# Three PSUM tiles of one bank for the seven-product projections of a hybrid decoder layer

## The chip, the cores and the metric

The kernel runs on one core of a Trainium2 chip. The core has a matrix engine (TensorE, "PE" in the profile, with its weight loads as "PEld"), VectorE ("DVE"), ScalarE ("ACT"), GpSimd ("POOL") and SyncE ("SP"), which here issues every DMA transfer. Each engine works through its own queue of instructions in order; semaphores make one engine wait for another. The metric is the device time of one execution in microseconds, and it is compared by the median of several executions.

## What is computed

One decoder layer on x of 1024 tokens by 1024 features, all in float32, with two token mixers side by side:

```
h      = RMSNorm(x)
q | k | v | z_a | xBC | z_s | dt | gate_logits = h @ w_in
y_a    = differential_attention(q, k, v) * silu(z_a)          # 1024 wide
y_s    = group_norm(state_space(conv(xBC), dt) * silu(z_s))   # 2048 wide
merged = sigmoid(g_a) * (y_a @ w_proj_attn) + sigmoid(g_s) * (y_s @ w_proj_ssd)
out    = x + merged @ w_out
```

The change concerns the line of `merged`: a product with K = 1024 (attention rows) and one with K = 2048 (state-space rows), each gated, then added.

## The kernel before, in words

Every float32 operand of a large product is split into a high and a low part (ScalarE copies the high part, VectorE or GpSimd subtracts it to get the low one), and three matmuls, high by high, high by low and low by high, replace one (`steps3`). Work before the projections is not touched by the change: eight attention heads, four state-space groups, then `gates`, which writes tanh(g/2) of all gate logits to memory (`gt_d`). Since sigmoid(g) is (1 + tanh(g/2)) / 2, gating a block is one VectorE instruction, (gate + 1) * sum.

**The projections** (`products`). The K of 3072 rows is taken in three chunks of 1024, c = 0, 1, 2: attention, then the two halves of the state-space rows. Within a chunk the 1024 output features are taken in four pairs of 128 (ob = 0, 2, 4, 6), and the tokens in two halves. So a pair is a product of a 2x2 block matrix of weights with a 2x2 block matrix of activations. It is computed with seven block products instead of eight, in the order b11, t2, b21, t3, t1, t4, b22 with the numbers 1, 6, 2, 7, 5, 4, 3 (`ORDER`). A block product is 4 blocks of K by 3 matmuls, 12 matmuls of 128 by 128 by 512, and a pair has 84. The products go to three accumulators in PSUM, `into = {1: x, 6: y, 2: x, 7: y, 5: z, 4: y, 3: z}`; a PSUM bank holds 128 x 512 float32, one accumulator. Before, x and y are the two halves of one tile of two banks (`pxy`), and z is a tile of one bank (`pz`). The order of the tile framework's waits goes by tiles: an instruction that writes any part of a tile waits for the earlier readers of that tile.

After each product `pair_step` does its part of the sums: product 1 is copied to SBUF (`pc`, ScalarE); u6 = pc + y, u7 = pc + y (VectorE, L1288); x after product 2 is output block (0,0); u7 + z is block (1,1) (`c22`, L1295); pc + y after product 4 is block (1,0); u6 + z after product 3 is block (0,1). `BEFORE` names which of these must have been planned before a product may be issued: the copy before product 2, u6 before product 7, u7 before product 4, c22 before product 3. `out_block` then gates the block with a gate loaded from `gt_d` (L1319, tile `gl`), adds for c = 1, 2 what the earlier chunks left in memory (`acc_d`, tile `ac`, the add on GpSimd except in the last pair, L1323), and stores it to `acc_d`; in the last pair of c = 2 it splits it for the output product instead. `pair_loads` issues the loads of gates and old sums at 2.0, 7.5, 10.2 and 12.9 us of planned time into a pair.

**Weights** (`pair_splits`). Each pair needs seven weight combinations. GpSimd forms four sums and differences of raw blocks (tiles `s3`, `rawp`), and each of the seven is split: copies on ScalarE, subtractions on VectorE except two on GpSimd (s3 and the last). Tiles `wp`, nine of them, so weights are split more than a pair ahead.

**Activations** (`prepare`, `sums_of`, `fill`). Sums and differences of the y rows are made on GpSimd once per chunk and kept in memory (`t_d`); `fill` loads 28 pieces per chunk and splits each (ScalarE and VectorE) into a "form" (tiles f0b, f1t and so on, or pieces of hH and hL, which held h before). There is room for 31 forms, and a chunk's forms are given free while its last pair (ob = 6) is computed. So 25 of the next chunk's 28 loads and splits fall into the last pair of one chunk and the first of the next.

**What sets the order.** The kernel is written as generators that a planner (`Plan`) runs in the order of a planned time. Each instruction adds an assumed cost to its engine's clock (`mm`, `act`, `tt`, `stt`, `load`), and a task goes on when its inputs are ready by that clock. The result is a fixed order of instructions per engine; the real waits are those of the tiles. `Slots` count buffers: `scs`, `mms` and `trs` are the three PSUM pools of two tiles each (`pxy` came from `scs`, `pz` from `mms`; `trs`, one bank each, were free at this stage).

After the projections `final` multiplies the merged blocks (`mg`, split by `split_mg`) with w_out into tiles `po` and adds x.

## Time and profile before

| | |
|---|---|
| median of three executions | 1723.9 us (1723.13 to 1725.33) |
| profiled execution | 1722.27 us |
| its span, first to last instruction | 1720.5 us |
| TensorE busy | 1649.6 us, 96% |
| VectorE, ScalarE, GpSimd busy | 1095.6, 814.6, 595.4 us |
| gates end, projections begin | 1338.7 us |
| projections c = 0, 1, 2 | 90.6, 98.8, 99.1 us |
| last matmul of the projections, end of span | 1627.2, 1720.5 us |

The profile gives each engine's busy time, and with every wait what ended it. In a timeline row stand the start and length in microseconds, the engine, the line, the operation with its output and inputs, the number of instructions merged into the row, and in brackets the idle time before it with its releaser. A matmul takes 0.39 us from start to end, but one starts about every 0.23 us, so TensorE's busy share hides short stops; the start times do not.

### The profile page before, as it was taken

To read this page: it belongs to the slowest core of one execution; us is meant where nothing else is said; L and a number is where in the kernel's file an instruction comes from. 1 tells how busy PE (TensorE), PEld (TensorE's weight loads), DVE (VectorE), ACT (ScalarE), POOL (GpSimd) and SP (SyncE) were. 2 spreads that over 40 slices of the span, in tenths; PEclk is the share of its full clock that TensorE was granted. 3 is DMA by queue.
4 is the path that set the end of the run, shared out by engine and by line. 5 is a ranking of instruction groups with operands and counts; after the bars stand their busy time and mean duration, and the time that the engine had idled before them with its cause. 6 is when DMAs were issued, how large, how long until landed. Compare 5 with 4: busy or idle time off the path is not lost. (4 is left out here: it accounts for less than half of the span.)

```text
span 1720.5 us, 23583 instructions
## 1 busy us (share of the span) xinstructions
PE 1649.6 (96%) x8226; PEld 1364.5 (79%) x8226; DVE 1095.6 (64%) x1878; ACT 814.6 (47%) x1967; POOL 595.4 (35%) x656
## 2 busy tenths in 40 slices
PE   7999999999999999999999999999999888877899
PEld 5788888888888888888888888888788666665787
DVE  6676676677676635788588489466641658586621
ACT  5646556556565533564565365255442424142310
POOL 4323233233232210233333233167645344656200
PEclk9999999999999999999999999999999999999999
DMA  6202022021120121321422233077695657586732
GB/s 186 62 10 62 7 56 62 7 56 32 31 62 7 56 68 49 98 80 44 122 80 62 91 100 80 19 227 262 222 339 187 222 192 264 189 281 202 243 130 68
DMA packets 171044, 198.66 MB, mean 115 GB/s; under 512 B 11813, under 2 KB 114990, under 8 KB 170926
## 3 DMA queue, kind: packets, MB, share of 16 engines
q1 hardware_dynamic: 170926, 197.16, 36.0%
q8 instruction: 65, 1.06, 0.3%
q14 instruction: 53, 0.43, 0.1%
HBM read 147.71 MB, written 49.41 MB: 115 GB/s over the span
## 5 line engine op out<-in xcount | busy, mean ns | idle before, releaser
L165 PE MATMUL pma<-w,hH 128*128 128x512 f32 x1024 | 343.4, 405 | 0.2 <-ACT hH L189 0.2
L165 PE MATMUL pc<-hH,w 128*128 128x512 f32 x768 | 243.7, 394 | 0.0
L165 PEld LDWEIGHTS pma<-w,hH 128*128 128x128 f32 x1024 | 189.6, 190 | 34.6 <-ACT hH L189 0.6
L165 PE MATMUL pma<-w,hL 128*128 128x512 f32 x512 | 206.6, 404 | 0.0
L189 ACT ACTIVATE w<-raw 128x512 fp32r<-128x512 f32 (+1 forms) x194 | 120.5, 625 | 125.5 <-PE pc L165 46.3
L194 POOL TENSOR_TENSOR w<-raw,w 128x512 fp32r<-128x512 f32 (+1 forms) x62 | 83.8, 1352 | 260.9 <-ACT w L189 255.6
L165 PE MATMUL pmz<-w,hH 128*128 128x512 f32 x512 | 165.4, 397 | 0.0
L165 PEld LDWEIGHTS pc<-hH,w 128*128 128x128 f32 x768 | 142.9, 188 | 28.2
L165 PE MATMUL pg<-hH,w 128*128 128x512 f32 x512 | 161.9, 393 | 0.0
L194 DVE TENSOR_TENSOR w<-raw,w 128x512 fp32r<-128x512 f32 x132 | 111.1, 848 | 69.6 <-ACT w L189 66.4
L165 PE MATMUL pc<-hL,w 128*128 128x512 f32 x384 | 151.7, 395 | 0.0
L189 ACT ACTIVATE p<-p,nm 128x256 f32<-128x256 f32 (+7 forms) x128 | 98.2, 769 | 46.2 <-DVE nm L645 46.2
L189 ACT ACTIVATE wp<-rawp 128x512 fp32r<-128x512 f32 x72 | 45.1, 631 | 156.4 <-PE pxy L165 82.9
L165 PEld LDWEIGHTS pg<-hH,w 128*128 128x128 f32 x512 | 95.8, 188 | 19.2
L165 PEld LDWEIGHTS pma<-w,hL 128*128 128x128 f32 x512 | 97.2, 190 | 16.9 <-DVE hL L194 0.3
L165 PEld LDWEIGHTS pmz<-w,hH 128*128 128x128 f32 x512 | 94.8, 188 | 18.2
L165 PE MATMUL pmz<-w,hL 128*128 128x512 f32 x256 | 101.0, 395 | 0.0
L165 PE MATMUL pg<-hL,w 128*128 128x512 f32 x256 | 100.9, 394 | 0.0
L199 DVE SCALAR_TENSOR_TENSOR cv<-pc,cols,cv 128x1023 f32<-128x1023 f32 (+2 forms) x72 | 91.8, 1275 | 12.2 <-ACT cv L189 11.5
L645 DVE CUSTOM_DVE_ANT_0 p<-sc,maskb 128x256 f32<-128x256 f32 (+7 forms) x128 | 91.5, 752 | 12.2 <-PE sc L165 11.6
L221 POOL TENSOR_TENSOR f<-ssv,e 128x1 f32<-128x1 f32 x64 | 13.7, 214 | 245.0 <-ACT av L189 245.0
L189 ACT ACTIVATE ab<-ab,nac 128x128 f32<-128x128 f32 x256 | 77.9, 390 | 28.1 <-POOL ab L934 28.1
(252 smaller groups left out, 3628.3 us busy)
## 6 DMA issues: line engine op xcount, KB each, us to landing
raw<-in_w_in_dram SPq DMA_DIRECT2D x176, 256.0 KB, 3.1
ab<-act_d SPq DMA_DIRECT2D x32, 512.0 KB, 5.4
t_d<-ts SPq DMA_DIRECT2D x24, 512.0 KB, 3.4
gl<-gt_d SPq DMA_DIRECT2D x48, 256.0 KB, 4.4
acc_d<-gl SPq DMA_DIRECT2D x44, 256.0 KB, 2.2
ys_d<-xdt SPq DMA_DIRECT2D x32, 256.0 KB, 2.5
gt_d<-gt SPq DMA_DIRECT2D x32, 256.0 KB, 5.4
ts<-ys_d SPq DMA_DIRECT2D x16, 512.0 KB, 5.9
```

The costliest lines, as they stand in the source:

```text
L165: nc.tensor.matmul(o, lhsT=lhsT, rhs=rhs, start=start, stop=stop, **kw)
L189: nc.scalar.activation(o, i, f, **kw)
L194: (nc.vector if eng == "V" else nc.gpsimd).tensor_tensor(out=o, in0=a, in1=b, op=op)
L199: nc.vector.scalar_tensor_tensor(out=o, in0=a, scalar=s, in1=b, op0=op0, op1=op1)
L221: nc.gpsimd.tensor_tensor(out=dst, in0=src, in1=add, op=ALU.add)
L645: nc.vector.tensor_tensor_reduce(out=p[:, 0:n], in0=sc[:, 0:n], in1=maskb[:, S - n:S], scale=-1.0, scalar=3e38, op0=ALU.add, op1=ALU.min, ...
```

## The change

The accumulators x, y and z become three tiles of one bank each: X from `trs`, Y from `mms`, Z from one half of a tile of `scs`. The sums that complete a block are written back to the accumulator in PSUM instead of to SBUF for c = 1, 2: c22 goes to X (after block (0,0) has been gated), block (1,0) to Y, (0,1) to Z; each accumulator is given free after its last gating.

The order of the chunks changes: the two halves of the state-space rows are c = 0 and 1, the attention rows c = 2. For c = 0 nothing is gated and no gate is loaded: the four raw sums are stored to `acc_d` (block (0,0) through a ScalarE copy). For c = 1 the old sum is added and the result gated, once for both halves. For c = 2 the block is gated and the old sum added. The add of the old sum is on VectorE always. The subtraction for the weight s3 moves from GpSimd to VectorE.

The planner's assumed costs change from the projections on: 0.0135 us instead of 0.003 beside a matmul's columns, and 2.5 us instead of 0.8 from a transfer's end to its use. `prepare` no longer waits for the attention rows (they are done long before) but for the first state-space groups.

```diff
+    lag = [0.003, 0.8]
...
-            c = max(n / 2400 + 0.003, 0.057 if m <= 64 else 0.107)
+            c = max(n / 2400 + lag[0], 0.057 if m <= 64 else 0.107)
...
-        return pl.op("D", n, q + 0.6) + 0.8
+        return pl.op("D", n, q + 0.6) + lag[1]
...
-    for src, r0 in ((w_pa, 0), (w_ps, 0), (w_ps, 1024)):
+    for src, r0 in ((w_ps, 0), (w_ps, 1024), (w_pa, 0)):
...
-        t = yield from split(s3, t3, "G")
+        t = yield from split(s3, t3, "V")
...
     def products(c):
         for ob in range(0, 8, 2):
             ids = w_next(7)
-            ks = yield from pl.get(scs)
-            kz = yield from pl.get(mms)
-            sc, z = sct(f"pxy{c}{ob}"), mmt(f"pz{c}{ob}")
-            x, y = sc[:, 0:512], sc[:, 512:1024]
+            ks = []
+            for q in (trs, mms, scs):
+                ks.append((yield from pl.get(q)))
+            x, y, z = trt(f"pX{c}{ob}"), mmt(f"pY{c}{ob}"), sct(f"pZ{c}{ob}")[:, 0:512]
             into = {1: x, 6: y, 2: x, 7: y, 5: z, 4: y, 3: z}
-            cell = {"kc": (yield from pl.get(mids))}
-            pl.spawn(pair_loads(c, ob, cell))
+            cell = {"kc": (yield from pl.get(mids)), "x": x, "ks": ks}
+            if c:
+                pl.spawn(pair_loads(c, ob, cell))
...
         elif p == 2:
-            yield from out_block(c, ob, 0, 0, ps, cell, at)
+            if c:
+                yield from out_block(c, ob, 0, 0, ps, cell, at)
+            else:
+                k = yield from pl.get(mids)
+                o = midt(name=f"o{c}{ob}")
+                at = act(o, ps, AF.Copy, at)
...
         elif p == 5:
...
-            cell["c22"] = at = tt(u, u, ps, ALU.add, max(at, t))
-            yield from out_block(c, ob, 1, 1, u, cell, at)
-            mids.give(k, cell["done", 1, 1])
+            if c == 0:
+                cell["c22"] = at = tt(u, u, ps, ALU.add, max(at, t))
+                yield at
+                at = load(acc_row(ob + 1, 1), u, at)
+                mids.give(k, at)
+                return
             while ("done", 0, 0) not in cell:
                 yield pl.t + 0.1
+            cell["c22"] = at = tt(cell["x"], u, ps, ALU.add, max(at, t, cell["done", 0, 0]))
+            mids.give(k, at)
+            yield from out_block(c, ob, 1, 1, cell["x"], cell, at, (trs, kx))
         else:
...
+            k0, r, h, q, kq = (None, 1, 0, mms, ky) if p == 4 else ("u", 0, 1, scs, kz)
+            u, k, t = (cell["c"], cell["kc"], cell["ct"]) if p == 4 else cell["u", 6]
+            o = ps if c else u
+            at = tt(o, u, ps, ALU.add, max(at, t))
...
-        at = stt(gt, gt, 1.0, src, ALU.add, ALU.mult, at)
+        if c == 1:
+            at = tt(ps, ps, ac, ALU.add, at)
+            at = stt(gt, gt, 1.0, ps, ALU.add, ALU.mult, at - HOP)
+        else:
+            at = stt(ps, gt, 1.0, ps, ALU.add, ALU.mult, at)
+            at = tt(gt, ps, ac, ALU.add, at - HOP)
         cell["done", r, h] = at
-        if c:
-            yield at
-            at = tt(gt, gt, ac, ALU.add, at, "V" if c == 2 and ob == 6 else "G")
...
         yield from gates()
+        lag[:] = [0.0135, 2.5]
         for c in range(3):
             yield from products(c)
```

Three places show how the change moves instructions. Names are tiles with a number; wp is a split weight, f1b, f1t, hH and hL are forms, and what stands in brackets is what the instruction waits for.

TensorE, a quiet pair of c = 1 (ob = 2), the end of product 1, products 6 and 2, and the start of product 7, before:

```order
L165 MATMUL pxy_14069<-f1b_13668,wp_13853 128x512 x3
L165 MATMUL pxy_14069<-f1t_13676,wp_13884 128x512
L165 MATMUL pxy_14069<-f1t_13676,wp_13884 128x512 [waits Activation_49]
L165 MATMUL pxy_14069<-f1t_13676,wp_13884 128x512
L165 MATMUL pxy_14069<-f1t_13682,wp_13884 128x512 x3
L165 MATMUL pxy_14069<-f1t_13693,wp_13884 128x512 x3
L165 MATMUL pxy_14069<-f1t_13703,wp_13884 128x512 x3
L165 MATMUL pxy_14069<-f1b_13709,wp_13919 128x512 x2
L165 MATMUL pxy_14069<-f1b_13709,wp_13919 128x512 [waits DVE_49]
L165 MATMUL pxy_14069<-f1b_13716,wp_13919 128x512 x3
```

The same pair now:

```order
L167 MATMUL pX_14043<-f1b_13643,wp_13828 128x512 x3
L167 MATMUL pY_14044<-f1t_13651,wp_13862 128x512 x3
L167 MATMUL pY_14044<-f1t_13657,wp_13862 128x512 x3
L167 MATMUL pY_14044<-f1t_13665,wp_13862 128x512 x3
L167 MATMUL pY_14044<-f1t_13675,wp_13862 128x512 x3
L167 MATMUL pX_14043<-f1b_13681,wp_13894 128x512 [waits Activation_49]
L167 MATMUL pX_14043<-f1b_13681,wp_13894 128x512 x2
L167 MATMUL pX_14043<-f1b_13687,wp_13894 128x512 x3
L167 MATMUL pX_14043<-f1b_13695,wp_13894 128x512 x3
L167 MATMUL pX_14043<-f1b_13705,wp_13894 128x512 x3
L167 MATMUL pY_14044<-f1t_13711,wp_13919 128x512 [waits DVE_49]
```

The wait for ScalarE's copy of product 1 moved from product 6 to the start of product 2, and the wait for VectorE's u6 from product 2 to the start of product 7: each now has a whole product in front of it. The order of the products is the same.

GpSimd, about the same pair, before:

```order
L194 TENSOR_TENSOR rawp_14041<-rawp_14041,rawp_14042 128x4x128 [waits DMAHW3_49,Pool_49]
L194 TENSOR_TENSOR gl_14141<-gl_14141,ac_14143 128x512 [waits DMAHW3_49,DVE_49]
L194 TENSOR_TENSOR rawp_14041<-rawp_14041 128x4x128 [waits DVE_49,Pool_49]
L194 TENSOR_TENSOR gl_14165<-gl_14165,ac_14167 128x512 [waits DMAHW6_49,DVE_49]
L194 TENSOR_TENSOR gl_14188<-gl_14188,ac_14190 128x512 [waits DMAHW1_49,DVE_49]
L194 TENSOR_TENSOR rawp_14042<-rawp_14042,rawp_14041 128x4x128 [waits DVE_49,Pool_49]
L194 TENSOR_TENSOR wp_14276<-s_14194,wp_14276 128x512 [waits Activation_49]
L194 TENSOR_TENSOR gl_14249<-gl_14249,ac_14251 128x512 [waits DMAHW6_49,DVE_49]
L194 TENSOR_TENSOR wp_14336<-rawp_14042,wp_14336 128x512 [waits Activation_49]
```

Now, from one weight s3 to the pair's last split:

```order
L196 TENSOR_TENSOR s_14160<-rawp_14018 128x512 [waits DMAHW4_49,DVE_49]
L196 TENSOR_TENSOR rawp_14018<-rawp_14018,rawp_14019 128x4x128 [waits DMAHW5_49,Pool_49]
L196 TENSOR_TENSOR rawp_14018<-rawp_14018 128x4x128 [waits DVE_49,Pool_49]
L196 TENSOR_TENSOR rawp_14019<-rawp_14019,rawp_14018 128x4x128 [waits DVE_49,Pool_49]
L196 TENSOR_TENSOR wp_14307<-rawp_14019,wp_14307 128x512 [waits Activation_49]
```

The four adds of old sums and the split of s3 left GpSimd, which has five instructions per pair in place of ten.

VectorE, the pair ob = 4 of c = 1 from u6 on, before:

```order
L194 TENSOR_TENSOR u_14278<-pc_14258,pxy_14230 128x512
L199 SCALAR_TENSOR_TENSOR gl_14249<-gl_14249,pxy_14230 128x512
L194 TENSOR_TENSOR wp_14293<-rawp_14041,wp_14293 128x512
L194 TENSOR_TENSOR u_14317<-pc_14258,pxy_14230 128x512
L194 TENSOR_TENSOR wp_14314<-rawp_14042,wp_14314 128x512
L194 TENSOR_TENSOR u_14317<-u_14317,pz_14231 128x512
L199 SCALAR_TENSOR_TENSOR gl_14295<-gl_14295,u_14317 128x512
L194 TENSOR_TENSOR pc_14258<-pc_14258,pxy_14230 128x512
```

Now:

```order
L196 TENSOR_TENSOR u_14245<-pc_14226,pY_14198 128x512
L196 TENSOR_TENSOR wp_14243<-s_14160,wp_14243 128x512
L196 TENSOR_TENSOR pX_14197<-pX_14197,ac_14218 128x512
L201 SCALAR_TENSOR_TENSOR gl_14217<-gl_14217,pX_14197 128x512
L196 TENSOR_TENSOR wp_14264<-rawp_14018,wp_14264 128x512
L196 TENSOR_TENSOR u_14288<-pc_14226,pY_14198 128x512
L196 TENSOR_TENSOR wp_14286<-rawp_14019,wp_14286 128x512
L196 TENSOR_TENSOR pX_14197<-u_14288,pZ_14199 128x512
L196 TENSOR_TENSOR pX_14197<-pX_14197,ac_14259 128x512
L201 SCALAR_TENSOR_TENSOR gl_14258<-gl_14258,pX_14197 128x512
L196 TENSOR_TENSOR pY_14198<-pc_14226,pY_14198 128x512
```

The adds of the old sums (ac) and the split of s3 came in; a gating now has a PSUM operand where it had an SBUF copy, and the sum c22 (pX from u and pZ) stands behind the gating of block (0,0), whose two inputs gl and ac are loads.

More of the change, by code (lines that the diff above doesn't have):

```diff
@@ L1143, in y_rows @@
     def y_rows(c, kb):
-        return ya_d[kb * P:(kb + 1) * P] if c == 0 else ys_d[(c * 8 - 8 + kb) * P:(c * 8 - 7 + kb) * P]
+        return ya_d[kb * P:(kb + 1) * P] if c == 2 else ys_d[(c * 8 + kb) * P:(c * 8 + kb + 1) * P]
     def prepare():
-        while ready.get("ya", 0) < 2 * HEADS or ready["ya_at"] > pl.t:
+        while ready.get("ssd", {}).get(1, INF) > pl.t:
             yield pl.t + 0.5
         yield from sums_of(0)
-        while ("ssd", 1) not in ready:
-            yield pl.t + 0.5
-        yield from sums_of(1)
-        while ("ssd", GROUPS - 1) not in ready or ready["ssd", GROUPS - 1] > pl.t:
+        yield from sums_of(2)
+        while ready["ssd"].get(GROUPS - 1, INF) > pl.t:
             yield pl.t + 0.5
         pl.spawn(fill())
-        yield from sums_of(2)
+        yield from sums_of(1)
     def sums_of(c):
@@ L1261, in products @@
                 w_done(ids[n])
-                pl.spawn(pair_step(c, ob, p, into[p], cell, ks, kz), pe_done())
+                pl.spawn(pair_step(c, ob, p, into[p], cell), pe_done())
     def pair_loads(c, ob, cell):
@@ L1266, in pair_loads, with acc_row, pair_step @@
             yield pl.t + d
-            grow = ob + r + (8 if c else 0)
-            km = yield from pl.get(mids, 2 if c else 1)
-            km = km if c else [km]
-            gt = midt(name=f"gl{c}{ob}{r}{h}")
+            grow = ob + r + (8 if c == 1 else 0)
+            km = yield from pl.get(mids, 2)
+            gt, ac = midt(name=f"gl{c}{ob}{r}{h}"), midt(name=f"ac{c}{ob}{r}{h}")
             t = load(gt, gt_d[grow * P:(grow + 1) * P, h * 512:h * 512 + 512])
-            ac = None
-            if c:
-                ac = midt(name=f"ac{c}{ob}{r}{h}")
-                t = load(ac, acc_d[(ob + r) * 256 + h * P:(ob + r) * 256 + h * P + P])
+            t = max(t, load(ac, acc_row(ob + r, h)))
             cell["g", r, h] = (gt, ac, km, t)
-    def pair_step(c, ob, p, ps, cell, ks, kz):
+    def acc_row(ob, h):
+        return acc_d[ob * 256 + h * P:ob * 256 + h * P + P]
+    def pair_step(c, ob, p, ps, cell):
         at = pe_done()
+        kx, ky, kz = cell["ks"]
         if p == 1:
@@ L1289, in pair_step @@
         elif p == 2:
-            yield from out_block(c, ob, 0, 0, ps, cell, at)
+            if c:
[4 more added lines that the diff above has]
+                at = act(o, ps, AF.Copy, at)
+                cell["done", 0, 0] = at
+                trs.give(kx, at)
+                yield at
+                at = load(acc_row(ob, 0), o, at)
+                mids.give(k, at)
         elif p == 5:
@@ L1327, in out_block @@
         else:
-            at = load(acc_d[(ob + r) * 256 + h * P:(ob + r) * 256 + h * P + P], gt, at)
+            at = load(acc_row(ob + r, h), gt, at)
             if c == 2:
```

32 lines of the change are left out of this document (15 added, 17 removed).

## The prediction

> **What bounds the kernel now.** First the page's busy shares, then the busy times by stage and by pair of output blocks, then the timeline of one quiet pair, last the waits. In a window row stand length, busy time (and instructions) of PE, PEld, DVE, ACT and POOL, granted clock, DMA share, GB/s. The first three rows are the chunks c=0, 1, 2 of the seven-product projections; the others are pairs, from the first of c=0 to the last of c=2.
>
> ```profile
> PE 1649.6 (96%) x8226; PEld 1364.5 (79%) x8226; DVE 1095.6 (64%) x1878; ACT 814.6 (47%) x1967; POOL 595.4 (35%) x656
> ...
> 1338.70:1429.30 90.60, 79.94 (x339) 62.39 (x338) 62.61 (x78) 36.46 (x65) 34.84 (x24) 1.00 0.64 215
> 1429.30:1528.10 98.80, 82.54 (x342) 64.15 (x341) 70.32 (x85) 31.56 (x56) 55.73 (x39) 0.98 0.70 230
> 1528.10:1627.20 99.10, 82.50 (x331) 62.95 (x330) 67.69 (x82) 32.84 (x57) 49.56 (x33) 0.97 0.66 225
> ...
> 1338.70:1361.30 22.60, 19.97 (x86) 15.60 (x85) 20.81 (x27) 12.82 (x24) 8.10 (x6) 1.00 0.76 256
> 1361.30:1383.90 22.60, 19.90 (x86) 15.52 (x85) 11.03 (x15) 4.91 (x8) 8.79 (x7) 1.00 0.38 126
> 1429.30:1455.00 25.70, 21.74 (x87) 16.84 (x86) 21.14 (x29) 10.18 (x19) 10.19 (x8) 0.93 0.83 281
> 1455.00:1479.00 24.00, 19.65 (x84) 15.22 (x83) 15.70 (x20) 5.43 (x9) 14.75 (x10) 1.00 0.57 175
> 1503.00:1528.10 25.10, 21.13 (x90) 16.48 (x90) 20.99 (x24) 11.15 (x20) 15.51 (x12) 1.00 0.85 280
> 1528.10:1557.00 28.90, 20.85 (x78) 14.86 (x76) 26.11 (x29) 11.61 (x21) 16.33 (x11) 0.94 0.78 269
> 1557.00:1582.00 25.00, 22.25 (x94) 17.30 (x94) 16.00 (x19) 4.91 (x8) 15.76 (x11) 1.00 0.55 181
> 1605.00:1627.20 22.20, 20.37 (x88) 16.13 (x87) 15.57 (x25) 11.53 (x20) 5.14 (x4) 1.00 0.89 308
> ```
>
> TensorE sets the pace, and this stage, 288.5 us from 1338.7 to 1627.2, is where it has holes. What it needs at least comes from a product without a wait, in the chain that ended last; a pair in a timeline shows where a hole is.
>
> ```profile
> 1600.64 2.72 PE pxy L165 x12
> ```
> ```profile
> 1364.15 0.39 PE L165 MATMUL pxy<-f0t,wp 128*128 128x512 f32 x1
> 1364.88 0.58 ACT L189 ACTIVATE pc<-pxy 128x512 f32<-128x512 f32 x1
> 1365.52 2.79 PE L165 MATMUL pxy<-f0t,wp 128*128 128x512 f32 x11 [0.98 <-ACT pc L189]
> 1368.14 0.61 PE L165 MATMUL pxy<-f0b,wp 128*128 128x512 f32 x2
> 1368.87 0.69 DVE L194 TENSOR_TENSOR u<-pc,pxy 128x512 f32<-128x512 f32 x1 [3.16 <-PE pxy L165]
> 1369.61 2.57 PE L165 MATMUL pxy<-f0b,wp 128*128 128x512 f32 x10 [0.85 <-DVE u L194]
> 1372.01 0.61 PE L165 MATMUL pxy<-f0t,wp 128*128 128x512 f32 x2
> 1372.66 0.69 DVE L199 SCALAR_TENSOR_TENSOR gl<-gl,pxy 128x512 f32<-128x512 f32 x1 [3.11 <-PE pxy L165]
> 1373.50 1.86 PE L165 MATMUL pxy<-f0t,wp 128*128 128x512 f32 x7 [0.87 <-DVE gl L199]
> ```
>
> Twelve matmuls start in 2.72 us, 0.2267 each; a pair has 84, so 19.04 us, and the twelve pairs 1008, so 228.5. The stage **loses 60.0 us**. The timeline shows three stops per pair, none wanted by the algorithm: product 6, which goes to y, waits for ScalarE's copy of x; product 2, into x, waits for the DVE sum that reads y; product 7, into y, for the gating that reads x. Both accumulators are one tile pxy, and the dependency is held by the tile. The stops are 1365.52 - 1364.15 - 0.23 = 1.14, 1369.61 - 1368.37 - 0.23 = 1.01 and 1373.50 - 1372.24 - 0.23 = 1.03 us, 3.2 together; the matmuls behind a stop start 0.24 apart ((2.79 - 0.39) / 10), which is the other 0.4 of the pair's 22.6 - 19.04 = **3.56 us**. Twelve pairs: 42.7 of the 60.0. The other 17.3 are the rows longer than 22.6: 3.1 and 2.5 + 6.3 where one chunk's operands replace the other's, 1.4 in the quiet pair of c=1 shown (its neighbour is alike), 2.4 in one of c=2 and 0.4 in the next. In these quiet pairs the copy itself is late:
>
> ```profile
> 1584.18 1.15 ACT L189 ACTIVATE wp<-rawp 128x512 fp32r<-128x512 f32 x2 [5.58 <-POOL rawp L194]
> 1585.24 0.58 ACT L189 ACTIVATE pc<-pxy 128x512 f32<-128x512 f32 x1
> 1585.87 1.22 PE L165 MATMUL pxy<-hH,wp 128*128 128x512 f32 x2 [2.27 <-ACT pc L189]
> ```
>
> The copy is queued on ScalarE behind weight conversions, and these wait for POOL, where four adds of the old sums stand per pair in c=1 and 2.
>
> **Part 1, three tiles of one bank: -42.7.** In the new order every matmul that waits for ScalarE or VectorE has a whole other product (2.72 us) between it and the work that it waits for: the copy has product 6, the sums u6 and u7 have products 2 and 5, the sum that frees z has product 4. In the rows above the reader is done 0.9 to 1.3 us behind the last matmul (1364.54 to 1365.46 for the copy), so it is hidden with over 1 us to spare; without that cover the 1 us stops return. The bounds are 0 and 42.7; I take all of it.
>
> **Part 2, POOL's adds to VectorE, split of s3 too.**
>
> ```profile
> L194 POOL TENSOR_TENSOR gl<-gl,ac 128x512 f32<-128x512 f32 x14 | 21.3, 1530 | 14.8 <-DVE gl L199 14.8
> ...
> L199 DVE SCALAR_TENSOR_TENSOR gl<-gl,pc 128x512 f32<-128x512 f32 x4 | 5.8, 1462 | 0.0
> L194 DVE TENSOR_TENSOR u<-pc,pxy 128x512 f32<-128x512 f32 x8 | 5.5, 686 | 10.2 <-issue 5.3 <-PE pxy L165 4.8
> L194 DVE TENSOR_TENSOR hH<-ry1t,hH 128x512 fp32r<-128x512 f32 x4 | 2.7, 680 | 0.0
> ...
> L194 DVE TENSOR_TENSOR pS<-pS,pre x24: 681/691/700, 728.5 to 1225.7; 128x512 f32<-128x512 f32 x24
> ...
> 1530.87 0.60 DVE u L194
> ```
>
> POOL falls from ten operations per pair to five, so ScalarE's weight conversions there no longer wait behind adds, and the quiet pairs of c=1 and 2 should run like those of c=0: -1.4 x 2 - 2.4 - 0.4 = -5.6. A sum with a PSUM operand costs VectorE 0.69 (writing PSUM too, as pS does), 0.60 where one follows another; an operation with both inputs in SBUF costs the same alone but 1.46 on average beside POOL. c=0: 62.6 us for 78 operations, 12.7 over 0.64 each, by 24 on POOL: half a microsecond each. A quiet pair of c=1 or 2 now has 19 DVE operations, 19 x 0.60 + 5 x 0.5 = 14 of its 19 us: hidden.
>
> The rule against this is in the Trainium skill, "VectorE: DVE Perf Modes", Rules for kernel authors: copy a matmul's output to SBUF first if many operations follow. By it sums left in PSUM are the dear form, and the total could only be above mine. The trace disagrees: by the rows above the PSUM form is 0.69 always and the SBUF form 0.68 to 1.46, and the total keeps 0.60 in a queue.
>
> **Part 3, where the chunks change.** Here 25 forms (operands split in two) pass VectorE while gating runs. By the new order VectorE issues 58 operations over the two pairs at c=0/1 (53 before) and 63 at c=1/2 (51 before). With ten POOL operations at 0.5: 58 x 0.60 + 5 = 39.8 and 63 x 0.60 + 5 = 42.8, against 38.1 us of matmuls: late by 1.7 and 4.7. The transfers press too: the two rows about 1528.1 moved 280 x 25.1 + 269 x 28.9 = 14.8 MB; in 38.1 us that is 388 GB/s, where the highest 20 us row of the trace has 369.
>
> ```profile
> 1260.00:1280.00 20.00, 20.00 (x90) 16.57 (x89) 10.84 (x12) 10.79 (x18) 9.65 (x7) 1.00 1.03 369
> ```
>
> At 369 they need 40.1, late by 2.0 beside the 4.7. The bounds: 0, if weights (split a pair ahead) give way in the queue; and today's 11.9 with 17 more operations at 0.69, 24. I take 2.5 and 5, near the worked rows, and 0.25 for each of the other eight pairs: **9.5 us stay lost of 60.0**. Nothing else on the path is added: c=0 loses its gate loads and gating, and its one extra ScalarE copy takes 0.58 in a queue that is under a third busy there; order of the chunks and later landing times (2.5 for 0.8) only move queue entries.
>
> The clock: after the longest waits it is lower, for some 3 us.
>
> ```profile
> 1534.00:1538.00 4.00, 0.27 (x2) 1.00 0.54 198
> 1538.00:1542.00 4.00, 4.00 (x11) 0.57 0.90 308
> ```
>
> In the pairs at 0.93 and 0.94 above that is 1.8 + 1.7 us, already among the 11.9; I expect one such drop at c=1/2, within the 5. The Trainium skill ("TensorE: Matmul & The Clock Gate", Part 1) gives an idle window of about 3.4 us for it: by that rule waits of 1 to 2 us leave the clock alone, and the term would be 1.7 less.
>
> **Part 4, the tail.** From the stage's end to the span's end it is 93.3 us now.
>
> ```profile
> 1634.15 1.92 PE L165 MATMUL po<-w,hL 128*128 128x512 f32 x6 [1.79 <-ACT hL L189]
> ...
> 1634.15 83.17 PE po L165 x387
> ```
>
> The last pair's VectorE work (15.6 of 22.2 us above) must now end in 19: I add 1.0, between -1.8 (this wait gone) and +3 (the 3.2 us that the pair gets shorter).
>
> **Sum.** 1338.7 + 228.5 + 9.5 + 94.3 = 1671.0 span. The profiled execution is 1.8 above its span (1722.3 to 1720.5), the median 1.6 above that: **1674.4 us**, 49.5 less than 1723.9 (2.9%).
>
> **Rivals.**
> *All covered* (0.18): the chunk changes cost nothing and the po wait goes: 1338.7 + 228.5 + 91.5 + 3.4 = 1662. For it: c=0's first pair took 22.6 with 27 operations on VectorE. Against: 42.8 us of work in 38.1.
> *Queues bound at the chunk changes* (0.20): transfers and VectorE together, the 24 us of part 3, tail +2: 1338.7 + 228.5 + 24 + 95.3 + 3.4 = 1690. For it: DMA share 0.83 to 0.85 already there. Against: POOL's stretching halves.
> *The true waits take over* (0.08): the copy and sums late by over the 2.7 us of cover, as the 2.27 wait shows that ScalarE can be; if half of part 1 returns, 1674.4 + 21 = 1695. The change then does half of what it says. Against: c=0 never had it (0.98).
> *Slower* (0.04): a new chain. The sum that frees z for product 3 now stands behind the gating of block (0,0), and in c=1 and 2 that needs its two loads.
>
> ```profile
> gl<-gt_d SPq DMA_DIRECT2D x47, 256.0 KB, 4.4
> ...
> ac<-acc_d SPq DMA_DIRECT2D x31, 256.0 KB, 5.2
> ```
>
> Product 3 starts 6 x 2.72 = 16.3 us into a pair; three operations (2.1) before it leave 14.2, and the loads are issued at 2: it decides from a landing of 12 us, and a landing of 19 would cost 7 us in each of 8 pairs, 1674.4 + 56 = 1730. Against: the medians are less than half of 12.
>
> **How the numbers follow.** The forecast has 0.50. The range 1662 to 1695 reaches over the rivals but the last. A median here can tell 0.2% from no change; only the last rival can come out there or above: faster 0.95, same 0.01, slower 0.04.
>
> **What would show it.** Part 1: quiet pairs of 19.0 to 19.4 us in all chunks, with the 0.98, 0.85 and 0.87 us of idle time gone. Part 2: POOL under 30 us in each chunk (20 operations, today 24 take 34.8 in c=0), DVE's PSUM sums at 0.69. Part 3: the pairs at c=0/1 and 1/2 over 38.1 by 2.5 and 5. Part 4: po no earlier than 94 us before the end. Wrong if quiet pairs stay above 20, or if the chunk changes lose over 20.

## The result, and the profile after

The changed kernel takes **1678.97 us** (median of four runs, 1677.29 to 1681.57) against 1723.69 for the kernel before (four runs beside it, 1723.13 to 1725.33): a ratio of **0.974 [0.9723, 0.9757]**, 44.7 us less. The forecast was 1674.4, with a range of 1662 to 1695. The profiled execution, the fastest of the four, took 1677.29 us with a span of 1675.5 us (before 1722.27 and 1720.5).

First the busy shares on the page of the changed kernel.

```profile
PE 1638.2 (98%) x8226; PEld 1364.6 (81%) x8226; DVE 1084.8 (65%) x1902; ACT 815.9 (49%) x1971; POOL 530.5 (32%) x616
```

TensorE does the same 8226 matmuls in a span that is 45.0 us shorter. GpSimd lost 40 operations and 65 us. VectorE got 24 operations more and is busy 11 us less.

The busy times by stretch, columns as in the prediction: the chunks c = 0, 1, 2; two quiet pairs (the second of c=0, the third of c=1); the last pair of c=0 and the first of c=1; the last of c=1 and the first of c=2; the last pair of c=2; the tail.

```profile
1338.55:1414.70 76.15, 76.15 (x337) 63.08 (x336) 48.18 (x69) 37.73 (x68) 27.50 (x20) 1.00 0.60 202
1414.70:1504.96 90.26, 80.35 (x337) 64.62 (x336) 74.63 (x104) 33.24 (x58) 30.58 (x22) 0.96 0.81 275
1504.96:1583.77 78.81, 77.29 (x338) 62.76 (x336) 65.73 (x97) 31.57 (x54) 19.58 (x15) 1.00 0.75 252
1357.60:1376.60 19.00, 19.00 (x85) 15.76 (x84) 8.11 (x12) 5.41 (x9) 7.16 (x6) 1.00 0.34 113
1457.90:1476.90 19.00, 19.00 (x85) 15.76 (x84) 12.72 (x19) 4.92 (x8) 6.42 (x5) 1.00 0.68 225
1395.70:1414.70 19.00, 19.00 (x85) 15.74 (x84) 14.96 (x22) 13.77 (x26) 6.77 (x5) 1.00 1.00 342
1414.70:1438.85 24.15, 20.25 (x86) 15.46 (x84) 24.08 (x32) 10.92 (x20) 8.45 (x6) 1.00 0.89 298
1476.90:1504.96 28.06, 22.05 (x85) 17.64 (x84) 22.18 (x34) 12.60 (x22) 8.74 (x6) 0.88 0.93 328
1504.96:1526.64 21.68, 20.16 (x86) 15.46 (x85) 21.51 (x32) 10.76 (x19) 6.68 (x5) 1.00 0.88 291
1564.73:1583.77 19.04, 19.04 (x86) 15.77 (x84) 16.73 (x27) 10.98 (x19) 2.60 (x2) 1.00 0.97 340
1583.77:1675.50 91.73, 88.06 (x409) 73.14 (x407) 23.25 (x35) 8.01 (x13) 3.90 (x3) 1.00 0.35 119
```

A quiet pair now takes 19.0 us where it took 22.6 to 25.0: TensorE is busy in all of it. c=0 has no hole (76.15 for four pairs of 19.04). The stage from 1338.55 to 1583.77 lasts 245.2 us, 43.3 less than before, and loses 16.7 over the 228.5 that its matmuls need. All of that lies in three pairs: 5.1 in the first pair of c=1, 9.0 in the last of c=1, 2.6 in the first of c=2. The tail lasts 91.7 us, 1.6 less than before.

What TensorE waits for from the projections on, in the changed kernel (microseconds in total, times, longest; the largest three):

```profile
PE pY L167 <- DVE u L196: 8.2, 4, 6.0
PE pZ L167 <- DVE pX L196: 1.4, 2, 0.8
PE pX L167 <- ACT pc L191: 1.1, 1, 1.1
...
```

Before, there was a stop in every pair for the copy, for u6 and for a gating. What is left is mostly the wait for u6 or u7 at the two chunk changes, with one long instance.

At the change from c=0 to c=1 the waits in TensorE's timeline of the changed kernel are:

```profile
1421.42 3.01 PE L167 MATMUL pX<-f1b,wp 128*128 128x512 f32 x12 [1.11 <-ACT pc L191]
1425.20 3.01 PE L167 MATMUL pY<-f1t,wp 128*128 128x512 f32 x12 [0.76 <-DVE u L196]
...
1432.12 0.98 PE L167 MATMUL pY<-hL,wp 128*128 128x512 f32 x3 [1.19 <-DVE u L196]
...
1436.01 0.93 PE L167 MATMUL pZ<-hL,wp 128*128 128x512 f32 x3 [0.83 <-DVE pX L196]
```

These are the waits that the algorithm wants (copy before product 2, u6 before 7, u7 before 4, c22 before 3), each with a whole product as cover and still too late. VectorE is busy 24.08 of this pair's 24.15 us: it is the bound here. The first wait, for ScalarE's copy, leads back to it as well: the copy stood behind a weight conversion that waited 3.21 us for GpSimd, and GpSimd had waited 1.89 us for a weight subtraction on VectorE. In the pair ahead of this one VectorE was busy 14.96 of 19.00.

At the change from c=1 to c=2 the long wait is seen with VectorE's and ScalarE's rows:

```profile
1489.85 0.84 PE L167 MATMUL pZ<-hH,wp 128*128 128x512 f32 x3
1490.12 2.49 DVE L196 TENSOR_TENSOR f2b<-ry2b,f2b 128x512 fp32r<-128x512 f32 x4
...
1493.03 1.25 ACT L191 ACTIVATE f2t<-ry2t 128x512 fp32r<-128x512 f32 x2 [0.98 <-DMA ry2t<-t_d]
...
1493.69 2.36 DVE L196 TENSOR_TENSOR f2t<-ry2t,f2t 128x512 fp32r<-128x512 f32 x2 [1.08 <-ACT f2t L191]
...
1495.97 0.67 DVE L196 TENSOR_TENSOR u<-pc,pY 128x512 f32<-128x512 f32 x1
...
1496.70 1.65 PE L167 MATMUL pY<-hL,wp 128*128 128x512 f32 x3 [6.01 <-DVE u L196]
```

Product 5 ends at 1490.7, and product 4 waits 6.01 us for u7 (tile u). u7 is one VectorE instruction of 0.67 us whose inputs were there at 1488.0, when product 7 ended. In the 8.0 us from there to its start VectorE worked through nine instructions ahead of it in its queue, eight of them subtractions for the next chunk's forms. It was idle for only 1.08 us of this, where a form (f2t) waited for ScalarE, which waited for a transfer. So u7's place in the queue makes it late, more than a late operand does. Behind the wait the clock is lower, in the same kernel:

```profile
1496.70:1502.00 5.30, 5.30 (x13) 4.14 (x14) 2.68 (x4) 0.26 (x1) 0.48 (x1) 0.50 1.07 371
```

That is 5.3 us at 0.50, some 2.6 us of the 9.0 that this pair loses.

### The profile page after: what moved, and what is told of

Same layout as the page of the kernel before. It is cut to its first block, busy times and chain, and to the rows that moved or that the text cites. A ratio compares the mean times of both kernels' runs of the same rounds, so it can differ in the third digit from the quotient of the medians.

```text
span 1675.5 us, 23517 instructions
## 1 busy us (share of the span) xinstructions
PE 1638.2 (98%) x8226; PEld 1364.6 (81%) x8226; DVE 1084.8 (65%) x1902; ACT 815.9 (49%) x1971; POOL 530.5 (32%) x616
## 4 chain that ended last, share of the span: by engine, by line
PE 82%; DVE 5%; POOL 4%; issue 4%; ACT 3%; DMA 2%; SPq 0%; POOLq 0%; DVEq 0%; ACTq 0%
PE pma L167 17%; PE pc L167 15%; PE pmz L167 9%; PE pg L167 7%; PE po L167 5%; PE pY L167 4%; PE sc L167 4%; PE av L167 4%; PE pX L167 3%; PE pD L167 3%; PE pZ L167 2%; PE pa L176 2%; POOL ts L196 1%; ACT qh L191 1%; PE pS L167 1%
## 5 line engine op out<-in xcount | busy, mean ns | idle before, releaser
L167 PEld LDWEIGHTS pmz<-w,hH 128*128 128x128 f32 x512 | 94.8, 188 | 18.3
L647 DVE CUSTOM_DVE_ANT_0 p<-sc,maskb 128x256 f32<-128x256 f32 (+7 forms) x128 | 91.5, 752 | 12.2 <-PE sc L167 11.6
```

What stands on the lines that cost most here:

```text
L167: nc.tensor.matmul(o, lhsT=lhsT, rhs=rhs, start=start, stop=stop, **kw)
L647: nc.vector.tensor_tensor_reduce(out=p[:, 0:n], in0=sc[:, 0:n], in1=maskb[:, S - n:S], scale=-1.0, scalar=3e38, op0=ALU.add, op1=ALU.min, ...
```

## The experiments

Each is the changed kernel with one edit, except the first. Beside the median stands the length of the stage, from the first matmul into the first x to the first into `po`, read from the timeline of the kernel's profile: the stage begins at another time in each run, 1337.6 to 1341.0 us, and the stage is free of that. A ratio is to runs of the kernel before that were made beside the experiment (medians 1723.35 to 1725.89), so where kernels of different rows are close, the intervals of their ratios decide.

| kernel | median us (lowest to highest) | ratio to before | stage us |
|---|---|---|---|
| before | 1723.69 (1723.13 to 1725.33) | | 288.5 |
| after | 1678.97 (1677.29 to 1681.57) | 0.974 [0.9723, 0.9757] | 245.2 |
| 1 tiles only | 1683.43 (1682.82 to 1685.31) | 0.976 [0.9746, 0.9775] | 249.3 |
| 2 shared tile | 1744.37 (1743.37 to 1746.31) | 1.0113 [1.0098, 1.0128] | 310.4 |
| 3 old landing time | 1683.25 (1682.31 to 1684.26) | 0.9757 [0.9743, 0.9772] | 249.5 |
| 4 s3 on GpSimd | 1678.0 (1676.2 to 1678.48) | 0.9728 [0.9712, 0.9744] | 244.3 |
| 5 no low halves on VectorE | 1673.23 (1671.77 to 1673.77) | 0.9705 [0.969, 0.9719] | 237.7 |
| 6a landing 4.0 | 1683.33 (1682.31 to 1684.79) | 0.9765 [0.9751, 0.978] | 250.1 |
| 6b landing 5.5 | 1697.22 (1694.4 to 1699.98) | 0.9845 [0.9828, 0.9862] | 267.1 |
| 7 dearer VectorE | 1682.66 (1681.63 to 1683.88) | 0.9759 [0.9742, 0.9775] | 250.2 |
| 8 narrow gates | 1678.11 (1676.83 to 1679.25) | 0.9737 [0.972, 0.9753] | 244.1 |
| 9 last pair kept | 1677.12 (1675.81 to 1678.54) | 0.9731 [0.9717, 0.9746] | 244.6 |
| 10 kept, s3 on GpSimd | 1678.3 (1677.81 to 1680.18) | 0.974 [0.9725, 0.9755] | 246.7 |
| 11 eight adds fewer | 1673.8 (1672.82 to 1676.18) | 0.9716 [0.9703, 0.9729] | 241.6 |

A stage is that of one profile, and the low clock moves it by a microsecond and more: behind the long wait of c=1 it covers 5.8 us of matmuls in the changed kernel, but 2.9 in experiment 4, 3.5 in 8 and 3.7 in 11. Stages that differ by less than that are not told apart.

### 1 and 2: what is the tile split worth, alone and taken back?

Experiment 1 is the kernel before with the three accumulators in three tiles, each given free by itself, and nothing else:

```diff
-            sc, z = sct(f"pxy{c}{ob}"), mmt(f"pz{c}{ob}")
-            x, y = sc[:, 0:512], sc[:, 512:1024]
+            x, y, z = trt(f"pX{c}{ob}"), mmt(f"pY{c}{ob}"), sct(f"pZ{c}{ob}")[:, 0:512]
```

> The kernel before with one edit: the accumulators x, y, z are three tiles of one bank (chunk order, gating on every chunk, the adds on GpSimd and the planner's costs stay). Theory: the shared tile cost 3.56 us per pair, 42.7 in all, and the late copies of c=1, 2 (5.6) are covered too, since a whole product stands before each wait; the chunk changes get tighter by about 5. So 1723.7 - 43 to 1723.7 - 34: 1681 to 1690. Rival A (the gain is in the order of the queues, set by the planner's costs and the chunk order): above 1705. Rival B (the gain is in GpSimd's relief): above 1705, with the copy of product 1 late by 2.3 us in c=1, 2 as before.

Experiment 2 is the changed kernel with x and y back in the halves of one tile (z in `mms`), everything else as changed:

```diff
-            x, y, z = trt(f"pX{c}{ob}"), mmt(f"pY{c}{ob}"), sct(f"pZ{c}{ob}")[:, 0:512]
+            sc, z = sct(f"pxy{c}{ob}"), mmt(f"pz{c}{ob}")
+            x, y = sc[:, 0:512], sc[:, 512:1024]
```

> The changed kernel with X and Y as halves of one tile of two banks again and Z a tile of one bank, all else as changed. Theory: three stops of about 1 us come back in each of twelve pairs, +42.7 at most; the 16.7 us that the changed kernel's projections still lose at the chunk changes get smaller because VectorE has 22.6 instead of 19.0 us per pair: 1705 to 1722. Rival A and B: within 10 us of the changed kernel's 1679.

The split alone came out as expected: 1683.4, stage 249.3, so 39.2 of the stage's 43.3 us. All the rest of the change is worth the other 4.1; the intervals of the two ratios overlap. Its waits of TensorE, from the projections on (the two largest and the one for the copy):

```profile
PE pY L165 <- DVE u L194: 5.2, 5, 2.8
PE pZ L165 <- DVE u L194: 3.4, 2, 2.3
...
PE pX L165 <- ACT pc L189: 0.6, 1, 0.6
```

In the kernel before, the wait for the copy was the largest of its list:

```profile
PE pxy L165 <- ACT pc L189: 18.2, 12, 2.4
```

The wait for the copy, which came twelve times with up to 2.4 us each, is there once, with 0.6, although GpSimd still has its adds. All waits of the stage over 0.2 us lie between 1421 and 1437 and between 1494 and 1529, about the chunk changes, so the quiet pairs are free of them.

Experiment 2 missed. I had expected that the shared tile takes the split's gain back at most; it came out 18.5 us slower than the kernel before that ran beside it (1725.89). The rest of the change is good only with the split. A quiet pair of c=1 in experiment 2:

```profile
1463.60 2.79 PE L178 MATMUL pxy<-f1t,wp 128*128 128x512 f32 x11 [0.98 <-ACT pc L202]
...
1467.69 2.58 PE L178 MATMUL pxy<-f1b,wp 128*128 128x512 f32 x10 [0.85 <-DVE u L207]
...
1472.24 2.56 PE L178 MATMUL pxy<-f1t,wp 128*128 128x512 f32 x10 [1.52 <-DVE gl L212]
...
1478.54 0.73 PE L178 MATMUL pxy<-hL,wp 128*128 128x512 f32 x2 [0.79 <-DVE pxy L207]
...
1481.48 0.96 PE L178 MATMUL pxy<-hL,wp 128*128 128x512 f32 x3 [1.51 <-DVE gl L212]
...
1489.78 1.43 PE L178 MATMUL pxy<-f1t,wp 128*128 128x512 f32 x5 [0.98 <-ACT pc L202]
```

The first three stops are those of before. Two are new: a matmul into y waits for a sum that is now written into x, and for the gating that now reads x. The stop at 1472.24 is longer too (1.52 for 0.87 us), since the add of the old sum now comes ahead of the gating. The pair takes 1489.78 - 1463.60 = 26.2 us, where it took 22.6 to 25.0 before and 19.0 now. Keeping the sums in PSUM makes more readers and writers of each accumulator, and with a shared tile each of them stops its neighbour.

### 3 and 4: the new landing time and s3

```diff
-        lag[:] = [0.0135, 2.5]
```

> The changed kernel with the planner's old costs (0.003 us beside a matmul, 0.8 us after a transfer). Theory: only the order in the queues moves, and a quiet pair has over 5 us of idle VectorE, so quiet pairs stay at 19.0 to 19.5; the chunk changes, where VectorE and the transfers are full, can lose up to 10 more because loads count as landed too early: 1676 to 1692. Rival A (the planner's costs carry the gain): above 1700.

```diff
-        t = yield from split(s3, t3, "V")
+        t = yield from split(s3, t3, "G")
```

> The changed kernel with the split of the weight s3 on GpSimd again (0.60 us per pair less on VectorE, about 1.3 more on GpSimd, which stretches VectorE's SBUF operations by about 0.5). Theory: nothing of this is on the path in a quiet pair and the two effects cancel at the chunk changes: 1676 to 1682. Rival B: more than 1684, with ScalarE's weight conversions waiting for GpSimd again.

Both came within what was expected. The place of s3 makes no difference that can be measured. With the planner's old costs the kernel is 4.3 us slower by the medians and by the stage, though the intervals of the two ratios overlap, and the largest wait is another:

```profile
PE pZ L167 <- DVE pX L196: 7.7, 3, 5.0
...
```

This is product 3 waiting for c22 behind the gating of block (0,0): the mechanism of the prediction's slower rival, with 5.0 us in the first pair of c=2. The planned time of 2.5 us from landing to use keeps it at 1.4 in the changed kernel. It gains nothing at c=1/2, where the last pair of c=1 and the first of c=2 lose 9.5 us together with the old costs and 11.6 now. It gains in the last pair of c=2, which takes 23.6 us with the old costs and 19.0 now, and 1.2 us in the first pair of c=1.

### 5: is it VectorE at the chunk changes?

For c=1 and 2 ScalarE writes both halves of a form in one activation, and VectorE's subtraction for the low half is left out. The low half is then a second copy of the high one: this kernel leaves that part of the computation out.

```diff
-        t = act(form[0][:, 0], raw, AF.Copy, t)
-        yield t
-        t = tt(form[0][:, 1], raw, form[0][:, 0], ALU.subtract, t)
+        if c:
+            t = act(form[0], raw.unsqueeze(1).to_broadcast([P, 2, 512]), AF.Copy, t)
+        else:
+            ...
```

> The changed kernel, but for the chunks c=1, 2 the low part of the activation forms is written by ScalarE's one instruction together with the high part (both halves get the same copy), so that 56 VectorE subtractions are left out: the low part is not computed there. Transfers are the same. Theory: at c=0/1 VectorE is full (24.1 of 24.2 us in the first pair of c=1), at c=1/2 its queue holds sum u7 behind nine form subtractions that wait for late loads. Without them both losses (5.1 and 9.0 us) fall to 3 together: 1666 to 1671. Rival (the transfers themselves are too late, at 0.93 of their time): product 1 of the next chunk waits for its forms instead, 1676 to 1682.

The stage fell by 7.5 us, the median by 5.7, to 1673.2: between the range of the theory and that of the rival. The pair at c=0/1 is no longer held by VectorE:

```profile
1414.60:1436.00 21.40, 18.67 (x83) 15.14 (x82) 7.45 (x12) 21.40 (x27) 6.02 (x5) 1.00 0.92 322
```

VectorE is busy 7.45 us of it and ScalarE all of its 21.40: the work went to the engine that makes the copy, and the copy came late:

```profile
1425.16 3.01 PE L167 MATMUL pX<-f1b,wp 128*128 128x512 f32 x12 [2.73 <-ACT pc L191]
```

At c=1/2 u7 still makes TensorE wait, for another reason:

```profile
1494.25 0.69 DVE L196 TENSOR_TENSOR u<-pc,pY 128x512 f32<-128x512 f32 x1 [3.91 <-DMA acc_d<-gl]
...
1494.99 1.36 PE L167 MATMUL pY<-hL,wp 128*128 128x512 f32 x3 [4.26 <-DVE u L196]
```

Here u7 itself waited 3.91 us, for the buffer that it writes, which was still being stored. The last pair of c=1 and the first of c=2 lose 6.2 us together, for 11.6. So taking VectorE's work away helps, but the run doesn't say that VectorE is all of it: the transfers are late there too.

### 6 and 7: can the order alone be better?

A later planned landing puts u7 ahead of the forms in VectorE's queue. A dearer VectorE instruction in the planner spreads them. The edit of 6a stands here; 6b has 5.5 in the place of 4.0.

```diff
-        lag[:] = [0.0135, 2.5]
+        lag[:] = [0.0135, 4.0]
```

> The changed kernel with 4.0 us instead of 2.5 assumed from a transfer's end to its use; nothing but the order in the queues moves. In VectorE's queue 4 form subtractions, not 9, then stand between u6 and u7 in the last pair of c=1. Theory: the wait of 6.0 us and the slow clock behind it (some 8 us together) fall to 3 or less: 1671 to 1676. Rival (transfers late, whatever the order): 1677 to 1682.

> The same with 5.5 us: 3 form subtractions between u6 and u7 in the last pair of c=1. Theory: as with 4.0, 1670 to 1677; gates and old sums also count as later, so gatings stand later in the queue, which may cost 1 to 2 at product 3. Rival: 1677 to 1684.

```diff
-    lag = [0.003, 0.8]
+    lag = [0.003, 0.8, 0.07]
...
-        return pl.op(eng, 0.07 + 1.042e-3 * n if eng == "V" ...
+        return pl.op(eng, lag[2] + 1.042e-3 * n if eng == "V" ...
...
-        lag[:] = [0.0135, 2.5]
+        lag[:] = [0.0135, 2.5, 0.17]
```

> The changed kernel with 0.1 us more assumed for each sum or subtraction on VectorE from the projections on; only queue order moves. Five form subtractions stand between u6 and u7 in the last pair of c=1 instead of nine, six in the first of c=1 as before. Theory: the wait at c=1/2 falls by half, 1673 to 1677. Rival: 1677 to 1682.

All three missed: their medians are 4.4, 18.3 and 3.7 us above that of the changed kernel, and above the rival's range too. The last pair of c=1, the first of c=2 and the last of c=2 in 6a:

```profile
1476.37:1495.41 19.04, 19.04 (x85) 15.77 (x84) 16.93 (x25) 10.39 (x18) 6.99 (x5) 1.00 0.93 321
1495.41:1525.10 29.69, 23.06 (x86) 16.75 (x84) 26.60 (x41) 13.20 (x24) 8.98 (x7) 0.89 0.99 349
1563.19:1588.36 25.17, 21.15 (x86) 16.75 (x84) 17.25 (x28) 11.65 (x21) 2.59 (x2) 0.93 0.94 331
```

The last pair of c=1 loses nothing any more: u7 is in time there. (By the traces four form subtractions stand between u6 and u7 in this pair of 6a, and eleven, not nine, in that of the changed kernel.) But the first pair of c=2 loses 10.7 us, where it lost 2.6, and in 7 it loses 12.2. So at c=1/2 the order decides in which pair the loss shows and hardly how large it is: 10.7 and 12.2 us for 11.6, and 9.5 in experiment 3. What makes 6a and 7 slower lies elsewhere, in the last pair of c=2: it takes 25.2 and 24.6 us for 19.0, with a wait of 4.02 and 3.63 us for u7 and a low clock behind it. TensorE's waits in 6b (the largest two):

```profile
PE pY L167 <- DVE u L196: 6.7, 2, 4.0
PE pZ L167 <- DVE hH L196: 6.5, 6, 2.2
...
```

The forms themselves (hH, hL, f2b) are late now, in several places, and u still is. The clock adds to it: granted is 0.94 over the 267.1 us of this stage and 0.99 over the 245.2 of the changed kernel's, which by these figures is worth some 14 us at the most of the 21.9 that the stage is longer, since a low clock costs nothing while TensorE waits. By the landing time 0.8, 2.5, 4.0 and 5.5 the medians are 1683.3, 1679.0, 1683.3 and 1697.2. Of these four, 2.5 is best. Every order tried that served u7 of c=1 sooner served another instruction later.

### 8, 9 and 10: do the transfers bound it?

In experiment 8 a gate loads 128 of its 512 columns and is used four times over, so that three quarters of the gate bytes are left out (and the gates are not those of the reference):

```diff
-            t = load(gt, gt_d[grow * P:(grow + 1) * P, h * 512:h * 512 + 512])
+            t = load(gt[:, 0:P], gt_d[grow * P:(grow + 1) * P, h * 512:h * 512 + P], cols=512)
```

> The changed kernel with a quarter of each gate loaded (128 of 512 columns, used four times: three quarters of the gates are left out); the count of transfers and of instructions, the planner's costs and so the queue order stay, 0.2 MB less per gate, 1.6 MB less over the two pairs at c=1/2. Theory, as it stands after the earlier runs: at c=1/2 the transfers are full (361 GB/s, 1.00 of their time, behind the wait) and any order pays, so 1.6 MB at 0.36 to 0.39 MB/us buys 4 us of the 9.0 lost there; c=0/1, where VectorE is full, changes by 1 at most: 1673 to 1676. Rival (VectorE's queue alone): within 1.5 of 1679.

In experiment 9 the pairs of c=1 run in reverse order, and the four sums of each chunk's last pair stay in SBUF for the next chunk's first pair: 2 MB, eight transfers, less at each change. Experiment 10 is 9 with s3 on GpSimd, as in 4.

```diff
+    OBS = ((0, 2, 4, 6), (6, 4, 2, 0), (0, 2, 4, 6))
...
+        if c < 2 and ob // 2 * 2 == OBS[c][-1]:
+            held[c + 1, ob, h] = (tile_, k, at)
+            return
```

> The changed kernel with the pairs of c=1 in reverse order, so that the last pair of a chunk is the first of the next: its four sums stay in SBUF instead of going to memory and back, 2 MB and eight transfers fewer at each of the two changes; the result is complete. Theory: c=1/2 loses 3 to 5 instead of 9.0, c=0/1 as before 4 to 5: 1672 to 1676. Rival (VectorE's queue alone): 1678 to 1682; the four buffers that are held may make loads wait, which would show as later forms.

> The same with the split of the weight s3 on GpSimd, which alone gave 1678.0. Theory: 1 less than with the sums kept alone, where VectorE is full: 1671 to 1676. Rival: no difference or more, since GpSimd stretches VectorE's SBUF operations.

Experiment 8 went the rival's way: 1678.1, no difference. The wait for u7 is 5.68 us, and the stretch about it is as dense as it was:

```profile
1490.00:1505.00 15.00, 9.32 (x34) 7.26 (x33) 12.05 (x19) 7.38 (x13) 5.01 (x4) 0.77 1.03 363
```

DMA share 1.03 and 363 GB/s: from 1395 to 1560 us 5.0 MB less were moved (39.5 for 44.5 MB), but in this stretch other transfers took the place. Experiments 9 and 10 missed. 9, at 1677.1, lies between the two ranges, and can't be told from the changed kernel (the single runs overlap); 10, at 1678.3, went the rival's way. In 9 the wait for u7 did fall, and others came:

```profile
1494.44 0.98 PE L167 MATMUL pY<-hL,wp 128*128 128x512 f32 x3 [2.14 <-DVE u L196]
...
1523.12 0.73 PE L167 MATMUL pZ<-hL,wp 128*128 128x512 f32 x2 [2.17 <-DVE hL L196]
```

From 6.01 to 2.14 for u7, and in the next pair waits for forms, the largest 2.17. The last pair of c=1 loses 2.5 us and the first of c=2 7.0, 9.5 together instead of the 3 to 5 expected (experiment 9 changes the order as well as the bytes). By experiment 8, which leaves the order alone, fewer bytes alone don't shorten the changes.

### 11: fewer operations on VectorE, order and bytes as they are

The eight adds of the old sum in the first and in the last pair of c=1 are left out (their contribution is missing from the output). The planner still counts their time, so every other instruction keeps its place.

```diff
-            at = tt(ps, ps, ac, ALU.add, at)
+            if ob in (0, 6):
+                at = pl.op("V", 0.07 + 1.042e-3 * 512, at)
+            else:
+                at = tt(ps, ps, ac, ALU.add, at)
```

> The changed kernel without eight of VectorE's adds of the old sums: those of the first and the last pair of c=1 are left out (the loads stay, so the blocks of these pairs lack the chunk c=0). The order of all that is left is the same on every engine. Narrow gates moved nothing, so the theory is now that the count of VectorE operations ahead of the sums u6, u7 and c22 sets the loss at the changes: each add left out brings what stands behind it forward by 0.6 to 0.7. In the first pair of c=1 one add is ahead of u7 and c22: its 5.1 us of loss fall to 4.0 to 4.5; in the last, one is ahead of u7 (6.0 us of wait fall to 5.3) and three are ahead of the next pair, whose 2.0 fall to 0.5. Together 2.5 to 4 less: 1675 to 1676.5. Rival (late transfers hold the queue, VectorE has idle time to give): 1678.5 to 1679.5, pairs as before.

The three pairs at the changes in experiment 11:

```profile
1416.30:1438.54 22.24, 20.00 (x86) 15.53 (x84) 22.24 (x30) 11.16 (x20) 8.98 (x6) 1.00 0.90 313
1476.62:1504.59 27.97, 21.02 (x85) 16.93 (x84) 21.54 (x31) 12.69 (x22) 7.99 (x6) 0.88 0.92 329
1504.59:1524.59 20.00, 19.32 (x85) 15.69 (x84) 19.64 (x30) 10.72 (x19) 6.42 (x5) 1.00 0.92 310
```

The stage is 3.6 us shorter, within the 2.5 to 4 of the VectorE theory; the median fell by 5.2 us, to below the range expected. The two ranges of single runs don't overlap, though the intervals of the two ratios just do. Where the stage became shorter tells more: the first pair of c=1 takes 22.24 for 24.15 us, with VectorE busy in all of it, so its loss fell to 3.2, further than the 4.0 to 4.5 expected. The first pair of c=2 takes 20.00 for 21.68. These two changes, 1.9 and 1.7, are the whole 3.6. The last pair of c=1, where four adds are missing as well, takes 27.97 for 28.06. Its wait for u7 did not fall to 5.3 us: it grew from 6.01 to 6.95, and only the shorter stretch of low clock made up for it.

So VectorE's count of operations sets the loss at c=0/1, and part of it behind c=1/2. The 9.0 us in the last pair of c=1 don't follow the count. By experiments 3, 6a and 7 another order moves them into the next pair, and the two pairs still lose 9.5 to 12.2 us. What sets this sum, beyond the work on VectorE, stays open.

Of the kernels that compute everything none is clearly faster than the changed one: the lowest median among them is that of experiment 9, 1.9 us less, and its single runs overlap with those of the changed kernel.

## Why the prediction was right, and where not

**Part 1, -42.7 by three tiles: right.** The nine pairs away from the losses are at 19.0 to 19.1 us, within the 19.0 to 19.4 asked for, and the stops of 0.98, 0.85 and 0.87 are gone. The stage with the split alone loses 20.8 us where it lost 60.0. That is about 42.7 for the stops and 5.6 for the late copies of the quiet pairs, less 8.9 that the chunk changes lose more (20.8 for 11.9 before). I read this as the same work on the other engines, met sooner by a faster TensorE; it was not tried apart. Experiment 2 shows the mechanism from the other side. (The readers in the prediction's rows are done 0.92, 0.81 and 0.73 us behind the end of the last matmul, not 0.9 to 1.3; the cover of 2.72 us was enough either way.)

**Part 2, -5.6 by fewer operations on GpSimd: right in size, with the wrong reason.** The late copies are gone, but experiment 1 has GpSimd's adds as before and lost its late copies too. The product between copy and use gives enough cover for them. GpSimd is busy 27.5, 30.6 and 19.6 us per chunk, so c=1 is just above the limit of 30 that was foretold. The prices of the sums on VectorE are as foretold. Groups of VectorE in the stage, in the changed kernel:

```profile
L196 DVE TENSOR_TENSOR pX<-pX,ac 128x512 f32<-128x512 f32 x8 | 5.6, 696 | 2.6 <-PE pX L167 1.9 <-DMA ac<-acc_d 0.6
...
L201 DVE SCALAR_TENSOR_TENSOR pX<-gl,pX 128x512 f32<-128x512 f32 x8 | 5.5, 691 | 1.4 <-PE pX L167 1.3
```

And a gating with both inputs in SBUF, in the kernel before:

```profile
L199 DVE SCALAR_TENSOR_TENSOR gl<-gl,u 128x512 f32<-128x512 f32 x22 | 22.2, 1007 | 0.4
```

With a PSUM operand a gating takes 0.69 us, in the other form it took 1.01 on average. So "the total keeps 0.60 in a queue" held, except that an instruction that reads what the one before it wrote starts 0.72 us behind it (a gating behind its add, 1430.78 and 1430.06 in the changed kernel). It held against the rule of the Trainium skill ("VectorE: DVE Perf Modes", Rules for kernel authors) that the prediction names, to copy to SBUF first if many operations follow. By the rows of the chunks VectorE has 270 operations in the stage for 245, and is busy 188.5 us for 200.6.

**Part 3, 9.5 us of 60.0 stay lost: 16.7 did. This is the term that was mis-sized.** The work was sized well: VectorE is busy 14.96 + 24.08 = 39.0 us in the two pairs at c=0/1 (39.8 in the prediction) and 22.18 + 21.51 = 43.7 at c=1/2 (42.8). The step that failed is "late by 1.7 and 4.7", work less 38.1 us of matmuls over two pairs. It takes for granted that VectorE is never idle in the two pairs, so that its work only has to be set against their time. The changed kernel shows that it is idle: for 4.1 us of the two pairs at c=0/1 and 6.1 at c=1/2. Work and idle time together, less the 38.1, are what was lost, 5.1 and 11.6.

At c=0/1 the idle time is in the first of the two pairs: VectorE comes to the first form of the next chunk 6.9 us into it, and until then there is little for it to do. Its row in the changed kernel's timeline:

```profile
1402.58 0.68 DVE L196 TENSOR_TENSOR f1b<-ry1b,f1b 128x512 fp32r<-128x512 f32 x1
```

The second pair is full, so the loss is 24.15 - 19.04 = 5.1, against 2.5. At c=1/2 the loss is 9.0 and 2.6, against 5. Of the 6.1 us of idle time there 5.9 are in the first of the two pairs: 2.72 at 1502.23, where VectorE waits for product 4, which u7 and the low clock had held up; 1.08 ahead of f2t; and shorter ones. But by 6a and 7 u7's place is not what makes the sum of the two pairs large, so what does stays open at c=1/2.

The 0.25 us for each of the other eight pairs was too much: they lose nothing. (ScalarE is busy 36.46 of c=0's 90.60 us in the prediction's first row of the stage, 40% and not under a third; its extra copy cost nothing all the same.) The forecast took the order of the queues as given; by experiments 3, 6 and 7 other orders cost 4 to 18 us, in 3, 6a and 7 above all in the last pair of c=2 (4.6, 6.1 and 5.5 us), where the changed kernel loses nothing.

**Part 4, the tail: 91.7 for 94.3.** The sign was wrong. The wait of `po` for hL fell from 1.79 to 0.53, in the timeline of the changed kernel:

```profile
1589.22 1.91 PE L167 MATMUL po<-w,hL 128*128 128x512 f32 x6 [0.53 <-ACT hL L191]
```

The last pair's VectorE work (16.7 us in 19.0) did find its place, so the lower bound, -1.8, was nearer than the +1.0 taken.

**The sum.** 16.7 - 9.5 = 7.2 too little for the stage, 94.3 - 91.7 = 2.6 too much for the tail, and 0.15 for the start: 1671.0 becomes the 1675.5 of the span. The two errors have opposite signs and hide part of each other, so that the median came out 4.6 us from the forecast and not 7 is luck.

**The rivals.** *All covered* got the tail and c=0 right, and the changes wrong. *Queues bound*, with 24 us at the changes, is above the 16.7 measured; the place was right. *The true waits take over*: they do at the changes alone, by 3.9 us at c=0/1, not in the quiet pairs. *Slower*: the median landings of gates and old sums are 4.9 and 3.8 us, far under the 12 from which it decides, and the chain costs 1.4 us; with the old landing time it costs 7.7 (experiment 3), through VectorE's queue rather than through the loads.

**The clock.** One drop at c=1/2 was foretold, and there is one. The pair at c=0/1, with four waits of 0.76 to 1.19 us, kept 1.00. The Trainium skill ("TensorE: Matmul & The Clock Gate", Part 1) gives an idle window of about 3.4 us for a drop; the wait of 6.01 us and these four agree with it, but waits in other runs do not (last section).

## What to carry to other kernels

Two accumulators in one tile wait for each other's readers, whether the work needs it or not; look in the timeline for matmuls that wait right behind the first write into the other half, and give each accumulator its own tile before more readers are put on it, since without that the same readers cost more than they saved. When work is to be hidden in a stretch of some pairs, don't set the sum of it against the sum of the time: ask for each pair when its operands come, and what stands in the queue behind an instruction that has to wait. Where one order only moves the loss from one pair to another, look for a gain in fewer operations on the engine that is full, as at c=0/1 here.
